# Expert rows gathered and scattered over all 128 partitions, in a mixture-of-experts kernel with streamed weights

## The chip, the cores and the metric

One core of a Trainium2 chip runs the program. The metric is device time in microseconds (us), the median of several executions. Engines: PE (TensorE, matrix products and transposes), ACT (ScalarE), DVE (VectorE), POOL (GpSimd), SP (SyncE, which here only issues DMAs). 16 DMA engines move all data between the chip's memory (HBM) and the on-chip buffer (SBUF, 128 partitions).

## The reference

A decoder layer on 1024 tokens of width 2048, in float32: input LayerNorm, a mixer (one projection, a causal convolution group and a pooling group, one projection out), LayerNorm, and a hierarchical mixture of experts (MoE), which is the part that the change touches:

```
expert = group*8 + top_i            # each token goes to 2 of 32 experts
hb = silu(xb @ w_gate[e]) * (xb @ w_up[e])   # 2048 -> 512, per expert
y  = hb @ w_down[e]                          # 512 -> 2048
out[token] += gate * y
h = layer_norm(alpha*h + out)
```

All 32 experts are used, so 32 x 12 pieces of weights of 1 MB have to be read from HBM.

## The kernel before

The program runs in three parts: the mixer (up to about 1080 us), the MoE, and the last sum and LayerNorm (from about 2175 us). The change lies in the MoE.

**Weights.** Each expert has 8 units of gate and up weights (`in_w_gu_dram`) and 4 of down weights (`in_w_dn_dram`), each a tile of 128 partitions x 2048 floats. SP loads them in the order in which PE uses them (`load_next`, L1571), into 16 slots: ten `er`, three `e2a`, and one each of `e2b`, `e2c`, `e2d` (NE2, L57). `free` (L1588) gives a slot to the next unit when PE has used it. A few tiles that are needed only later take one early unit each (`load_home`, FIRST and FIRST2, L59). An issue on SP also waits until an earlier transfer of SP's queue has landed.

**Rows.** The routing table `tabd` holds, for each expert, the token and the destination of each of its rows. `ent_load` (L1364) fetches a block's part of it as the tile `en`; `gather` (L1371) is an indirect DMA, issued by POOL, that reads the rows from `h1d` into a tile `xg`, one row of 8 KB to one partition; `scatter` (L1376) writes the finished rows to `yd`. Unfilled places carry an index out of bounds and move nothing. There are five tiles `xg` of 128 x 2048, used in turn.

**Blocks.** Experts are sorted by their number of rows, and position p of the program takes the expert of rank PERM[p] (L72), with blocks of fixed size for that rank (BLOCKS, L69): 35 blocks over 32 positions, of which 7 have 128 places, 8 have 96, 8 have 64, 3 have 48 and 9 have 32. (The first two positions, which have 64 places each, are among the 8.) So a gather names 128, 96, 64, 48 or 32 partitions.

**Steps.** `steps` (L1560) is the list that sets the order of everything: 16 half units G (gate and up) and 8 half units D (down) per position, 768 in all, the first 8 G of the next position ahead of the D of this one. At each step PE multiplies the weights with the block's transposed rows `xt`. A Part of 64 rows puts its two matmuls side by side in PE's columns, a Part of 32 rows its four (`Part.mm`, L1429). `x_quad` (L1462) transposes rows on PE, into a PSUM tile `ms`, which ACT or DVE copies to `xt`; `hidden` (L1479) applies silu and the gate; `y_out` (L1518) adds the two sums of the down product to the block's own rows in `xg`. `rows_out` (L1656) issues the gather for the block five ahead and then the scatter of the block that is done, both on POOL.

Of the kernel before, what the change touches and what calls it, by code (L numbers as in the profile page):

```python
# [26 lines left out]
NE = 32  # L27
# [15 lines left out]
NXG = 5  # L43
# [21 lines left out]
ROWS = {38: (3, 4)}  # L65
# [4 lines left out]
          + [((0, 128),)] * 4 + [((0, 96),)] * 7 + [((0, 64),)] * 5 + [((0, 48),)] * 3 + [((0, 32),)] * 8)  # L70
# [7 lines left out]
def trunk_kernel(ctx, tc, xcat, gin, bin_, grow, brow, w_in, b_in, conv_w, conv_b, cln_g, cln_b,  # L78
# [1234 lines left out]
    XG = {}  # L1313

    def xg_tiles(name, ids):
        p_ = pool(name, 1)
        for i in ids:
            XG[i] = p_.tile([P, D], F32, name=f"xg{i}")
# [4 lines left out]
    xg_tiles("xgp", (2, 3, 4))  # L1323
# [4 lines left out]
    xg_tiles("xgq", (0, 1))  # L1328
    xtp = pool("xtp", 3)
# [34 lines left out]
    def ent_load(e, start, n):  # L1364
        t = enp.tile([P, 4], I32, name="en", tag="en")
        v = tabv[start:start + n] if isinstance(start, int) else tabv[bass.ds(start, n)]
        v = v[:, e] if isinstance(e, int) else v[:, bass.ds(e, 1)].rearrange("r e c -> r (e c)")
        nc.sync.dma_start(t[:n], v)
        return t

    def gather(en, xg, n):  # L1371
        nc.gpsimd.indirect_dma_start(out=xg[:n], out_offset=None, in_=h1d,
                                     in_offset=bass.IndirectOffsetOnAxis(ap=en[:n, 0:1], axis=0),
                                     bounds_check=SEQ - 1, oob_is_err=False)

    def scatter(en, xg, n):  # L1376
        nc.gpsimd.indirect_dma_start(out=yd, out_offset=bass.IndirectOffsetOnAxis(ap=en[:n, 1:2], axis=0),  # L1377
                                     in_=xg[:n], in_offset=None, bounds_check=2 * SEQ - 1, oob_is_err=False)
# [36 lines left out]
    class Part:  # L1415
# [3 lines left out]

        def __init__(self, r0, n):  # L1420
            self.r0, self.n = r0, n
            c0 = r0 % P
            if n == 64:
                self.at = {(0, 0): c0, (1, 0): 64 - c0}
            else:
                o = 64 - c0
                self.at = {(0, 0): c0, (0, 1): c0 + 32, (1, 0): o, (1, 1): o + 32}

        def mm(self, bank, lhs, t, half, first, last):  # L1429
# [5 lines left out]
            for j, odd, h_ in sorted(order, key=lambda x: self.at[x[:2]]):  # L1435
                c = self.at[j, odd]
                nc.tensor.matmul(bank[c:c + self.n], lhs(h_)[:, self.r0:self.r0 + self.n],  # L1437
                                 t[:, h_ * 1024 + j * 512:h_ * 1024 + (j + 1) * 512],
                                 start=first and (self.n == 32 or half == 0), stop=last and half == 1)

        def sums(self, bank, j, odd=0):
            c = self.at[j, odd]
            return bank[c:c + self.n]

        def rows(self, t, c0=0, c1=512):
            return t[self.r0:self.r0 + self.n, c0:c1]

    class Block:
# [6 lines left out]

        def x_alloc(self):
            self.xt = xtp.tile([P, 16, P], F32, name="xt", tag="xt")
# [4 lines left out]
        def x_quad(self, q):  # L1462
            p_ = ms()
            m, nk = self.m, 16 // self.quads()
            pv = p_[:, :nk * m].rearrange("p (k n) -> p k n", k=nk)
# [3 lines left out]
            xv = self.xt[:, nk * q:nk * q + nk, :m]  # L1469
            if q % 2:  # L1470
                nc.vector.tensor_copy(xv, pv)
            else:
                nc.scalar.activation(xv, pv, AF.Copy)

        def gu(self, u, t, half):
            for part, bank in zip(self.parts, self.gb):
                part.mm(bank, lambda h_: self.xt[:, 2 * u + h_, :], t, half, u == 0, u == 7)

        def hidden(self):  # L1479

            m = self.m
            sg = hbp.tile([P, 512], F32, name="sg", tag="sg")
            ul = hbp.tile([P, 512], F32, name="dt", tag="dt")
            odd = [p_ for p_ in self.parts if p_.n == 32]
            for part, bank in zip(self.parts, self.gb):
                if part.n == 64:
                    nc.scalar.activation(part.rows(sg), part.sums(bank, 0), AF.Silu)
                else:
                    t = hbp.tile([P, 1024], F32, name="od", tag="od", bufs=1)
                    nc.scalar.activation(part.rows(t), part.sums(bank, 0, 1), AF.Copy)  # L1490
                    nc.scalar.activation(part.rows(t, 512, 1024), part.sums(bank, 1, 1), AF.Copy)
                nc.scalar.activation(part.rows(ul), part.sums(bank, 1), AF.Copy)
            for part, bank in zip(self.parts, self.gb):
                if part.n == 32:
                    nc.vector.tensor_tensor(part.rows(sg), part.rows(t), part.sums(bank, 0), op=OP.add)
                    nc.vector.tensor_tensor(part.rows(ul), part.rows(ul), part.rows(t, 512, 1024), op=OP.add)
            yield
            for part in odd:
                nc.scalar.activation(part.rows(sg), part.rows(sg), AF.Silu)
                yield  # L1500
            nc.vector.scalar_tensor_tensor(sg[:m], sg[:m], self.en[:m, 2:3].bitcast(F32), ul[:m],
                                           op0=OP.mult, op1=OP.mult)
            for _ in range(YX):
                yield
            p_ = ms()
            for k in range(4):
                nc.tensor.transpose(p_[:, k * m:(k + 1) * m], sg[:m, k * P:(k + 1) * P], ident[:m, :m])
            self.ht = hbp.tile([P, 512], F32, name="hth", tag="hth")
            nc.scalar.activation(self.ht[:, :4 * m], p_[:, :4 * m], AF.Copy)

        def down(self, u, t, half):

            m = self.m
            for part, bank in zip(self.parts, self.pds[u // 2]):
                part.mm(bank, lambda h_: self.ht[:, (2 * (u % 2) + h_) * m:(2 * (u % 2) + h_ + 1) * m], t, half,
                        u % 2 == 0, u % 2 == 1)

        def y_out(self, dp):  # L1518
            m, c = self.m, 1024 * dp
            t = hbp.tile([P, 512], F32, name="dt", tag="dt")  # L1520
            for part, bank in zip(self.parts, self.pds[dp]):
                xs = part.rows(self.xg, c, c + 512)
                nc.scalar.activation(part.rows(t), part.sums(bank, 1), AF.Copy)  # L1523
                if part.n == 32:
                    o = hbp.tile([P, 1024], F32, name="od", tag="od", bufs=1)
                    nc.scalar.activation(part.rows(o), part.sums(bank, 0, 1), AF.Copy)
                    nc.scalar.activation(part.rows(o, 512, 1024), part.sums(bank, 1, 1), AF.Copy)
                nc.vector.scalar_tensor_tensor(xs, xs, ALPHA / 2, part.sums(bank, 0), op0=OP.mult, op1=OP.add)  # L1528
                if part.n == 32:
                    nc.vector.tensor_tensor(xs, xs, part.rows(o), op=OP.add)  # L1530
                    nc.vector.tensor_tensor(part.rows(t), part.rows(t), part.rows(o, 512, 1024), op=OP.add)
            xs = self.xg[:m, c + 512:c + 1024]
            nc.vector.scalar_tensor_tensor(xs, xs, ALPHA / 2, t[:m], op0=OP.mult, op1=OP.add)  # L1533
# [3 lines left out]
    FIN = [(len(ALL) - 1 - d) % NXG for d in (4, 3)]  # L1537
    for m, (p, b) in enumerate(ALL):
        b.xg = XG[m % NXG]
    next_ent, next_gather = [0], [0]  # L1540

# [35 lines left out]
    def load_home(home):  # L1577
# [4 lines left out]
        t = xtp.tile([P, 2048], F32, name="xt", tag="xt") if home == "x" else XG[home]  # L1582
# [16 lines left out]
    def x_early(p):  # L1599

        return POS[p + 1][:3 - len(POS[p])] if p + 1 < NE else []
# [10 lines left out]
    nc.gpsimd.memset(XG[0], 0.0)  # L1612
    ents(2)
    gathers(1)
# [22 lines left out]
    def first_rows(ms_):  # L1637

        for m in ms_:
            nc.gpsimd.memset(XG[m], 0.0)  # L1640
            gathers(m + 1)

    first_rows((1, 2))
# [12 lines left out]
    def rows_out(p):  # L1656

        if p:
            gathers(ndone[0] + NXG)
        ndone[0] += len(POS[p])  # L1660
        for b in POS[p]:
            scatter(b.en, b.xg, b.n)
# [5 lines left out]
    for n, (kind, p, k) in enumerate(steps):  # L1668
        if n in ROWS:
            first_rows(ROWS[n])  # L1670
# [42 lines left out]
        while rows and (rows[0][0] <= n or n + 1 == len(steps)):  # L1713
            rows_out(rows.popleft()[1])
# [8 lines left out]
        if (kind, p, k) == ("D", NE - 2, 0):  # L1723
            nc.sync.dma_start(XG[FIN[0]], bc(lf_g, 0, D))
            nc.sync.dma_start(XG[FIN[1]], bc(lf_b, 0, D))
# [6 lines left out]
    with tc.For_i(0, nov, 1) as it:  # L1732
# [5 lines left out]
        blk.en, blk.xg, blk.gb, blk.pds = ent_load(e, st, P), XG[(len(ALL) - 1) % NXG], PB6[:2], [PB6[2:4], PB6[4:]]  # L1738
        gather(blk.en, blk.xg, P)
# [15 lines left out]
        scatter(blk.en, blk.xg, P)  # L1755
# [5 lines left out]
    fg, fb = XG[FIN[0]], XG[FIN[1]]  # L1761
# [160 lines left out]
```

## Time and profile before

| | us |
|---|---|
| median of 3 runs | 2276.13 (2275.77 to 2277.64) |
| the profiled execution | 2279.34 |
| its span, first to last instruction | 2277.5 |

The profiled execution's own time is 1.8 us more than its span and 3.2 us above the median of the runs.

The page of the profile gives busy times per engine, then the span in 40 slices of 57 us: a digit is the busy share in tenths, PEclk the granted TensorE clock in tenths of full speed, DMA the mean busy share of the 16 DMA engines, and GB/s what they moved. The view of stretches gives the same for any interval, and the view of waits says who waited for whom. In a row, `xg<-h1d,en` means that `xg` is written from `h1d` and `en`; `x16` is a count.

### The profile page before, as it was taken

How to read it: one execution, taken by the hardware profiler on the slowest of the kernel's cores; microseconds unless marked ns; L12 is line 12 of the kernel's file. 1: busy time of each engine (PE TensorE's matmuls, PEld its weight loads, DVE VectorE, ACT ScalarE, POOL GpSimd, SP SyncE). 2: the span in 40 equal slices, each digit the busy share in tenths (PEclk: the TensorE clock that was granted, in tenths of full speed). 3: DMA queues.
4: the chain of work that ended last, by engine and by line, in shares of the span. 5: the costliest groups of instructions: out<-in, count | busy, mean ns of one | idle time of the engine just before them, and what ended most of it. 6: DMA issues, size and time to landing. Idle time of an engine off the chain costs nothing. (4 is left out here: it accounts for less than half of the span.)

```text
span 2277.5 us, 29748 instructions
## 1 busy us (share of the span) xinstructions
PE 2011.4 (88%) x11015; PEld 1170.3 (51%) x11015; DVE 1130.0 (50%) x1918; ACT 746.1 (33%) x1308; POOL 670.7 (29%) x536
## 2 busy tenths in 40 slices
PE   5899999999999989987699999999979998999900
PEld 4799999978877867766232232223312222233300
DVE  8678767768856696796242212222111123131269
ACT  5633334324433444453112211222211122221255
POOL 5566757635222354264210001000000000000045
PEclk8999999999999999999799999999989998999955
DMA  6211121123565665678899999999999999989984
GB/s 206 96 56 56 56 66 56 56 79 104 208 199 166 226 224 210 218 261 306 310 374 416 405 393 393 400 413 411 356 399 398 408 416 392 402 323 418 420 329 163
DMA packets 132916, 614.29 MB, mean 270 GB/s; under 512 B 21216, under 2 KB 27872, under 8 KB 78368
## 3 DMA queue, kind: packets, MB, share of 16 engines
q1 hardware_dynamic: 124480, 570.37, 66.0%
q0 software_dynamic: 6848, 33.60, 4.2%
q10 hardware_dynamic: 1440, 8.39, 0.9%
q8 instruction: 88, 1.44, 0.3%
q14 instruction: 60, 0.49, 0.1%
HBM read 570.11 MB, written 51.36 MB: 273 GB/s over the span
## 5 line engine op out<-in xcount | busy, mean ns | idle before, releaser
L1437 PE MATMUL mm<-er,xt 128*64 128x512 f32 (+1 forms) x2120 | 420.7, 612 | 20.0 <-DMA er<-in_w_gu_dram 19.9
L754 PE MATMUL mm<-hl,whi 128*128 128x256 f32 (+2 forms) x1152 | 359.5, 324 | 0.6 <-POOL hl L343 0.6
L753 PE MATMUL mm<-hh,whi 128*128 128x256 f32 (+2 forms) x1152 | 347.3, 326 | 0.4 <-ACT l L589 0.4
L1528 DVE SCALAR_TENSOR_TENSOR xg<-xg,mm 64x512 f32<-64x512 f32 (+1 forms) x100 | 68.1, 681 | 515.6 <-ACT dt L1523 364.5
L373 POOL TENSOR_TENSOR wlo<-raw,whi 128x512 fp32r<-128x512 f32 x129 | 176.5, 1369 | 405.9 <-ACT whi L372 341.0
L1377 POOL DMA_INDIRECT yd<-xg,en x35 | 33.1, 945 | 798.3 <-DVE xg L1533 675.5
L758 PE MATMUL mm<-hh,wlo 128*128 128x256 f32 (+2 forms) x1152 | 258.1, 323 | 1.9 <-POOL wlo L373 1.9
L1437 PEld LDWEIGHTS mm<-er,xt 128*64 128x64 f32 (+1 forms) x2120 | 109.3, 128 | 275.1 <-issue 221.3
L372 ACT ACTIVATE whi<-raw 128x512 fp32r<-128x512 f32 x252 | 156.6, 627 | 271.3 <-PE mm L754 138.2
L412 DVE SCALAR_TENSOR_TENSOR ms<-l,cwt,ms 128x512 f32<-128x512 f32 x352 | 232.5, 749 | 0.0
L754 PEld LDWEIGHTS mm<-hl,whi 128*128 128x128 f32 x1152 | 219.0, 190 | 18.7 <-POOL hl L343 1.0
L753 PEld LDWEIGHTS mm<-hh,whi 128*128 128x128 f32 x1152 | 219.2, 190 | 3.4 <-ACT l L589 0.8
L758 PEld LDWEIGHTS mm<-hh,wlo 128*128 128x128 f32 x1152 | 193.6, 190 | 37.0 <-POOL wlo L373 2.9
L1437 PE MATMUL mm<-er,hth 128*64 128x512 f32 (+1 forms) x1032 | 201.9, 611 | 7.0 <-DMA er<-in_w_dn_dram 6.9
L1523 ACT ACTIVATE dt<-mm 64x512 f32<-64x512 f32 (+1 forms) x100 | 59.1, 591 | 364.7 <-PE mm L1437 350.9
L1219 PE MATMUL mm<-wlo,yh 128*128 128x512 f32 x392 | 156.2, 399 | 11.1 <-DVE wlo L373 10.9
L1218 PE MATMUL mm<-whi,yh 128*128 128x512 f32 x392 | 158.2, 404 | 1.6 <-ACT whi L372 1.6
L1220 PE MATMUL mm<-whi,yl 128*128 128x512 f32 x392 | 155.4, 396 | 0.0
L428 POOL TENSOR_TENSOR l<-l,t 128x512 f32<-128x512 f32 x112 | 141.8, 1295 | 0.0
L1437 PEld LDWEIGHTS mm<-er,hth 128*64 128x64 f32 (+1 forms) x1032 | 55.2, 129 | 152.9 <-issue 123.3
L373 DVE TENSOR_TENSOR wlo<-raw,whi 128x512 fp32r<-128x512 f32 x123 | 103.3, 851 | 56.6 <-ACT whi L372 54.9
L1437 PE MATMUL mm<-e2a,xt 128*64 128x512 f32 (+1 forms) x536 | 102.9, 599 | 1.1 <-DMA e2a<-in_w_gu_dram 1.1
(347 smaller groups left out, 2752.2 us busy)
## 6 DMA issues: line engine op xcount, KB each, us to landing
er<-in_w_gu_dram SPq DMA_DIRECT2D x161, 1024.0 KB, 19.8
er<-in_w_dn_dram SPq DMA_DIRECT2D x77, 1024.0 KB, 19.4
e2a<-in_w_gu_dram SPq DMA_DIRECT2D x47, 1024.0 KB, 20.7
raw<-in_w_out_dram SPq DMA_DIRECT2D x70, 512.0 KB, 4.4
raw<-in_w_in_dram SPq DMA_DIRECT2D x56, 512.0 KB, 3.3
e2a<-in_w_dn_dram SPq DMA_DIRECT2D x25, 1024.0 KB, 19.3
e2c<-in_w_gu_dram SPq DMA_DIRECT2D x16, 1024.0 KB, 20.6
e2d<-in_w_gu_dram SPq DMA_DIRECT2D x15, 1024.0 KB, 21.7
```

The costliest lines, as they stand in the source:

```text
L372: nc.scalar.activation(h, src, AF.Copy)
L373: self.lo(s).tensor_tensor(l, src, fr(h), op=OP.subtract)
L412: nc.vector.scalar_tensor_tensor(a, src, w, a, op0=OP.mult, op1=OP.add)
L428: nc.gpsimd.tensor_tensor(a, a, t, op=OP.add)
L753: nc.tensor.matmul(o, wh[:, ks], hh[q][:, kk, a0:a1], start=k == 0, stop=False)
L754: nc.tensor.matmul(o, wh[:, ks], hl[q][:, kk, a0:a1], start=False, stop=False)
L758: nc.tensor.matmul(o, wl[:, ks], hh[q][:, kk, a0:a1], start=False, stop=k == 15)
L1218: nc.tensor.matmul(po[t_], a_, wh, start=n == 0, stop=False)
L1219: nc.tensor.matmul(po[t_], a_, wl, start=False, stop=False)
L1220: nc.tensor.matmul(po[t_], b_, wh, start=False, stop=n == 15)
L1437: nc.tensor.matmul(bank[c:c + self.n], lhs(h_)[:, self.r0:self.r0 + self.n], t[:, h_ * 1024 + j * 512:h_ * 1024 + (j + 1) * 512], start=fi ...
L1528: nc.vector.scalar_tensor_tensor(xs, xs, ALPHA / 2, part.sums(bank, 0), op0=OP.mult, op1=OP.add)
```

## The change

Blocks of up to 64 places (m = 64 or 32) get narrow tiles `xgn` of 128 x 1024, three of them; larger blocks keep tiles `xgw` of 128 x 2048, also three. A narrow block's row is cut into f pieces, 2 for m = 64 and 4 for m = 32, and piece c of row r lies at partition c*m + r. `fetch` works out the indices f*index + c on DVE (tile `ex`), and then one gather names all 128 partitions and pieces of 4 or 2 KB. A 96-row block is gathered with 128 places, whose last 32 carry the out-of-bounds index. Blocks of 48 places now have 64. `x_quad` transposes 128 x 128 pieces in a narrow block (8 or 4 transposes in place of 16). `y_out` works on 64 partitions for a narrow block, and the 32-row Parts add their two halves in one pass (`added`). Gathers are issued every fourth step, at the earliest 8 steps after the scatter from the same tile, and for wide tiles not before step 42. The space that comes free holds a 17th weight slot `e2e`, and the wide tiles take three early units.

```diff
-NXG = 5
+NXW, NXN, NXG = 3, 3, 5
-NE2 = {"a": 3, "b": 1, "c": 1, "d": 1}
-FIRST, FIRST2 = ("a", "a", "a", "c", "d", "x"), ("b", "er", "er", 3, 4)
+NE2 = {"a": 3, "b": 1, "c": 1, "d": 1, "e": 1}
+FIRST, FIRST2 = ("a", "a", "a", "c", "d", "e", "x"), ("b", "er", "er", 0, 1)
-ROWS = {38: (3, 4)}
+WSTEP = 42
...
-    def gather(en, xg, n):
-        nc.gpsimd.indirect_dma_start(out=xg[:n], out_offset=None, in_=h1d,
-                                     in_offset=bass.IndirectOffsetOnAxis(ap=en[:n, 0:1], axis=0),
...
+    def gather(idx, xg, f=1):
+        nc.gpsimd.indirect_dma_start(out=xg[:, :D // f], out_offset=None,
+                                     in_=h1d if f == 1 else h1d.rearrange("t (c d) -> (t c) d", c=f),
+                                     in_offset=bass.IndirectOffsetOnAxis(ap=idx[:, 0:1], axis=0),
...
+        def added(self, bank):
+            o = hbp.tile([P, 512], F32, name="od", tag="od", bufs=1)
+            c = 64 - self.r0
+            nc.scalar.activation(self.pair(o), bank[c:c + 64], AF.Copy)
+            nc.vector.tensor_tensor(self.pair(o), self.pair(o), self.pair(bank), op=OP.add)
+            return self.rows(o), o[self.r0 + 32:self.r0 + 64]
...
         def x_quad(self, q):
+            if self.f == 1:
...
+            else:
+                m, nk = P, 4
+                pv = p_.rearrange("p (k n) -> p k n", k=nk)
+                xv = self.xt[:, 512 * q:512 * q + 512].rearrange("p (k n) -> p k n", k=nk)
...
         def y_out(self, dp):
+            a = ALPHA / 2
+            if self.f > 1:
+                part, bank, o = self.parts[0], self.pds[dp][0], 64 * dp
+                here, there = slice(o, o + 64), slice(64 - o, 128 - o)
+                xs = self.xg[here, :D // self.f]
+                t = hbp.tile([P, 512], F32, name="dt", tag="dt")
+                nc.scalar.activation(t[here], bank[there], AF.Copy)
+                xh = xs[:, (dp if self.f == 2 else 0) * 512:][:, :512]
+                nc.vector.scalar_tensor_tensor(xh, xh, a, bank[here], op0=OP.mult, op1=OP.add)
+                if self.f == 2:
+                    xo = xs[:, (1 - dp) * 512:][:, :512]
+                    nc.vector.scalar_tensor_tensor(xo, xo, a, t[here], op0=OP.mult, op1=OP.add)
+                else:
+                    nc.vector.tensor_tensor(xs, xs, t[here], op=OP.add)
+                return
...
+        def fetch(self):
+            self.idx = self.en
+            if self.f > 1:
+                self.idx = enp.tile([P, 2], I32, name="ex", tag="ex")
+                for c in range(self.f):
+                    nc.vector.tensor_scalar(self.idx[c * self.m:(c + 1) * self.m], self.en[:self.m, 0:2], self.f, c,
+                                            op0=OP.mult, op1=OP.add)
+            gather(self.idx, self.xg, self.f)
+            self.come = True
...
-    def gathers(upto):
+    def gathers(n, upto):
         while next_gather[0] < min(upto, len(ALL)):
             b = ALL[next_gather[0]][1]
-            gather(b.en, b.xg, b.n)
+            if sent.get(b.place, -99) + 8 > n or b.f == 1 and n < WSTEP:
+                return
+            if b.place not in sent:
+                nc.gpsimd.memset(b.xg, 0.0)
+            b.fetch()
+            sent[b.place] = NONE
...
     for n, (kind, p, k) in enumerate(steps):
-        if n in ROWS:
-            first_rows(ROWS[n])
+        if n % 4 == 2:
+            gathers(n, min(ndone[0] + NXG, next_ent[0]))
```

How the instructions move, first on POOL's queue around positions 11 to 14, in the middle of the MoE. A row is a source line, an operation, and out<-in with the shape of the output; `yd` is the target of a scatter. Before:

```order
L1372 DMA xg_10328<-h1d,en 96x2048
L1372 DMA xg_10329<-h1d,en 32x2048
L1377 DMA yd<-xg_10330,en 2048x2048
L1372 DMA xg_10330<-h1d,en 128x2048
L1377 DMA yd<-xg_10346,en 2048x2048
L1372 DMA xg_10346<-h1d,en 64x2048
L1377 DMA yd<-xg_10347,en 2048x2048
L1372 DMA xg_10347<-h1d,en 32x2048
```

The same blocks with the change:

```order
L1379 DMA xgw_10329<-h1d,en 128x2048
L1379 DMA xgn_10351<-h1d,ex 128x512
L1385 DMA yd<-xgn_10349,ex 4096x1024
L1379 DMA xgw_10330<-h1d,en 128x2048
L1385 DMA yd<-xgw_10328,en 2048x2048
L1379 DMA xgn_10349<-h1d,ex 128x1024
L1385 DMA yd<-xgn_10350,ex 4096x1024
L1379 DMA xgn_10350<-h1d,ex 128x512
```

The order is the same here; every gather now names 128 partitions, and those of narrow blocks have rows of 1024 or 512 floats.

On DVE, the last two `y_out` pairs before the overflow list's count (`novt`) is read, at the end of the MoE. Before:

```order
L1528 SCALAR_TENSOR_TENSOR xg_10330<-xg_10330,mm 32x512
L1530 TENSOR_TENSOR xg_10330<-xg_10330,od 32x512
L1531 TENSOR_TENSOR dt<-dt,od 32x512
L1533 SCALAR_TENSOR_TENSOR xg_10330<-xg_10330,dt 32x512
L1528 SCALAR_TENSOR_TENSOR xg_10330<-xg_10330,mm 32x512
L1530 TENSOR_TENSOR xg_10330<-xg_10330,od 32x512
L1531 TENSOR_TENSOR dt<-dt,od 32x512
L1533 SCALAR_TENSOR_TENSOR xg_10330<-xg_10330,dt 32x512
L1730 TENSOR_LOAD novt
```

With the change:

```order
L1564 SCALAR_TENSOR_TENSOR xgn_10350<-xgn_10350,mm 64x512
L1569 TENSOR_TENSOR xgn_10350<-xgn_10350,dt 64x512
L1564 SCALAR_TENSOR_TENSOR xgn_10350<-xgn_10350,mm 64x512
L1569 TENSOR_TENSOR xgn_10350<-xgn_10350,dt 64x512
L1807 TENSOR_LOAD novt
```

Two DVE instructions in place of four follow each half of the last block's down product; on ACT, one copy (L1562) takes the place of three (L1523, L1526, L1527).

On PE, the last position's transposes. Before:

```order
L1437 MATMUL mm<-e2a,xt 32x512 x8
L1468 MATMUL ms<-ident,xg_10330 128x32 x16
L1437 MATMUL mm<-e2c,xt 32x512 x4
L1437 MATMUL mm<-e2d,xt 32x512 x4
L1437 MATMUL mm<-e2b,xt 32x512 x4
```

With the change:

```order
L1447 MATMUL mm<-er,xn 32x512 x8
L1502 MATMUL ms<-ident,xgn_10350 128x128 x4
L1447 MATMUL mm<-er,xn 32x512 x12
L1447 MATMUL mm<-e2a,xn 32x512 x8
L1543 MATMUL ms<-ident,sg 128x32 x4
```

Four transposes of 128 x 128 stand where sixteen of 32 rows stood.

## Rows read from the trace of the kernel before

**Rows 1.** The page: DMA share in tenths and GB/s, in 40 slices.
```profile
DMA  6211121123565665678899999999999999989984
GB/s 206 96 56 56 56 66 56 56 79 104 208 199 166 226 224 210 218 261 306 310 374 416 405 393 393 400 413 411 356 399 398 408 416 392 402 323 418 420 329 163
```

**Rows 2.** Stretches of the MoE; columns as in the first line.
```profile
core 0: us, PE busy (x) PEld busy (x) DVE busy (x) ACT busy (x) POOL busy (x), PEclk, DMA share, GB/s
1104.00:1140.00 36.00, 36.00 (x178) 12.80 (x177) 4.69 (x7) 5.04 (x8) 2.30 (x3) 0.94 0.93 338
1140.00:1930.00 790.00, 735.67 (x4013) 222.13 (x4013) 183.41 (x327) 162.05 (x285) 54.53 (x55) 0.97 1.01 398
1930.00:2167.00 237.00, 227.67 (x1296) 73.92 (x1292) 52.33 (x79) 52.00 (x92) 10.53 (x11) 0.99 0.96 391
```

**Rows 3.** SP's waits for PE, 1140 to 1930 and 1930 to 2167.
```profile
SPq L1361 <- PE mm L1437: 11.9, 23, 2.3
...
SPq L1361 <- PE mm L1437: 135.3, 63, 5.8
```

**Rows 4.** PE's longest waits, 1104 to 2170: us, times, longest.
```profile
PE mm L1437 <- DMA er<-in_w_gu_dram: 19.9, 18, 4.3
PE ms L1507 <- DVE sg L1501: 11.7, 8, 3.3
```

**Rows 5.** Stretches: a 64-place gather, a scatter, a 128- and a 96-place gather.
```profile
1451.20:1455.00 3.80, 3.80 (x23) 0.93 (x20) 0.00 (x0) 0.00 (x0) 0.00 (x0) 1.00 1.06 250
1441.80:1445.40 3.60, 3.60 (x20) 0.85 (x21) 1.27 (x2) 1.20 (x3) 0.00 (x0) 1.00 1.00 419
1416.00:1421.00 5.00, 5.00 (x26) 1.71 (x24) 1.81 (x3) 1.12 (x2) 0.00 (x0) 1.00 1.01 419
1308.60:1314.00 5.40, 5.40 (x32) 1.45 (x28) 0.00 (x0) 0.39 (x1) 0.00 (x0) 1.00 1.04 267
```

**Rows 6.** POOL in order of time: the three gathers of group 5.
```profile
1304.27 0.97 POOL L1372 DMA_INDIRECT xg<-h1d,en  x1 [8.28 <-DMA yd<-xg,en]
...
1411.63 1.02 POOL L1372 DMA_INDIRECT xg<-h1d,en  x1 [7.35 <-DMA er<-in_w_gu_dram]
...
1446.92 0.95 POOL L1372 DMA_INDIRECT xg<-h1d,en  x1 [8.40 <-issue]
```

**Rows 7.** DMA queues from 1451.2 to 1455: packets, MB, share; q0 is POOL's.
```profile
q0 software_dynamic: 69, 0.40, 45.3%
```

**Rows 8.** Two stretches of the long middle, columns as in group 2.
```profile
1300.00:1425.00 125.00, 124.86 (x682) 38.04 (x684) 23.52 (x36) 23.67 (x42) 8.63 (x9) 1.00 1.01 394
1425.00:1720.00 295.00, 263.31 (x1420) 82.61 (x1417) 63.46 (x95) 58.42 (x102) 18.74 (x20) 0.95 1.01 397
```

**Rows 9.** PE in order of time: start, us; transposes, one wait.
```profile
1335.89 0.71 PE L1468 MATMUL ms<-ident,xg 64*128 64x64 f32 x8
...
1350.97 0.63 PE L1507 MATMUL ms<-ident,sg 128*128 128x128 f32 x4
...
2144.32 1.18 PE L1468 MATMUL ms<-ident,xg 32*128 32x32 f32 x16
...
2151.55 0.40 PE L1507 MATMUL ms<-ident,sg 32*128 32x32 f32 x4 [1.63 <-DVE sg L1501]
```

**Rows 10.** The end of the MoE in order of time: PE, ACT, DVE.
```profile
2167.70 2.42 PE L1437 MATMUL mm<-e2d,hth 128*32 128x512 f32 x8
...
2171.38 0.59 ACT L1527 ACTIVATE od<-mm 32x512 f32<-32x512 f32 x1
...
2174.03 0.68 DVE L1533 SCALAR_TENSOR_TENSOR xg<-xg,dt 32x512 f32<-32x512 f32 x1
```

**Rows 11.** The gathers, all 35: duration on POOL, and time to landing.
```profile
L1372 POOL DMA_INDIRECT xg<-h1d,en x35: 924/965/1402, 1094.4 to 2056.4; - x35
...
DMA to landing us min/median/max: 6.3/9.8/15.7
```

**Rows 12.** A small DVE instruction, 1082.59 us.
```profile
1082.59 0.16 DVE L1068 SCALAR_TENSOR_TENSOR ds<-rr,eid 128x4 int32<-128x4 f32 x1
```

More of the change, by code (lines that the diff above doesn't have):

```diff
@@ L1312, in trunk_kernel, with xg_tiles @@
     pool = lambda n_, b_: moe.enter_context(tc.tile_pool(name=n_, bufs=b_, reuse_waits="tile"))
-    XG = {}
-    def xg_tiles(name, ids):
+    XW, XN = {}, {}
+    def xg_tiles(name, to, n, w):
         p_ = pool(name, 1)
-        for i in ids:
-            XG[i] = p_.tile([P, D], F32, name=f"xg{i}")
+        for i in range(n):
+            to[i] = p_.tile([P, w], F32, name=f"{name}{i}")
     e2 = {"a": pool("e2a", NE2["a"])}
-    xg_tiles("xgp", (2, 3, 4))
+    xg_tiles("xgw", XW, NXW, D)
     e2["b"] = pool("e2b", NE2["b"])
@@ L1421, in __init__, with at, mm @@
             self.r0, self.n = r0, n
[L1422 to L1429, printed above, removed]
+        def at(self, j, odd=0, flip=0):
+            if self.n == 64:
+                return (self.r0 + 64 * j) % P
+            return (self.r0 + 64 * (odd ^ flip)) % P + 32 * j
+        def mm(self, bank, lhs, t, half, first, last, flip=0):
             if self.n == 64:
@@ L1483, in hidden @@
             ul = hbp.tile([P, 512], F32, name="dt", tag="dt")
-            odd = [p_ for p_ in self.parts if p_.n == 32]
+            both = {}
             for part, bank in zip(self.parts, self.gb):
@@ L1487, in hidden @@
                     nc.scalar.activation(part.rows(sg), part.sums(bank, 0), AF.Silu)
+                    nc.scalar.activation(part.rows(ul), part.sums(bank, 1), AF.Copy)
                 else:
[L1489 to L1496, printed above, removed]
+                    both[part] = part.added(bank)
             yield
-            for part in odd:
-                nc.scalar.activation(part.rows(sg), part.rows(sg), AF.Silu)
+            for part, (g_, u_) in both.items():
+                nc.scalar.activation(part.rows(sg), g_, AF.Silu)
+                nc.scalar.activation(part.rows(ul), u_, AF.Copy)
                 yield
@@ L1529, in y_out @@
-                if part.n == 32:
-                    nc.vector.tensor_tensor(xs, xs, part.rows(o), op=OP.add)
-                    nc.vector.tensor_tensor(part.rows(t), part.rows(t), part.rows(o, 512, 1024), op=OP.add)
-            xs = self.xg[:m, c + 512:c + 1024]
-            nc.vector.scalar_tensor_tensor(xs, xs, ALPHA / 2, t[:m], op0=OP.mult, op1=OP.add)
+                    y0, y1 = part.added(bank)
+                else:
+                    y0, y1 = part.sums(bank, 0), part.sums(bank, 1)
@@ new lines, in y_out @@
+                nc.scalar.activation(part.rows(t), y1, AF.Copy)
+                nc.vector.scalar_tensor_tensor(xs, xs, a, y0, op0=OP.mult, op1=OP.add)
+            xs = self.xg[:m, c + 512:c + 1024]
+            nc.vector.scalar_tensor_tensor(xs, xs, a, t[:m], op0=OP.mult, op1=OP.add)
+        def fetch(self):
[7 more added lines that the diff above has]
+            self.come = True
@@ L1535, in trunk_kernel, with send @@
+        def send(self):
+            scatter(self.idx, self.xg, self.m if self.f == 1 else P, self.f)
     POS = [[Block(*b) for b in ((FBLK,) if p < len(STAT) else BLOCKS[PERM[p]])] for p in range(NE)]
     ALL = [(p, b) for p in range(NE) for b in POS[p]]
-    FIN = [(len(ALL) - 1 - d) % NXG for d in (4, 3)]
-    for m, (p, b) in enumerate(ALL):
-        b.xg = XG[m % NXG]
+    ring = {}
+    for p, b in ALL:
+        w = b.f == 1
+        i = ring.get(w, 0)
+        b.place = (w, i % (NXW if w else NXN))
+        b.xg = (XW if w else XN)[b.place[1]]
+        b.come = False
+        ring[w] = i + 1
@@ L1540, in trunk_kernel @@
+    FIN = [XW[(ring[True] + d) % NXW] for d in range(2)]
+    SPARE = XW[(ring[True] + 2) % NXW]
     next_ent, next_gather = [0], [0]
+    sent = {}
     def ents(upto):
@@ L1635, in trunk_kernel @@
             b.x_quad(q)
[L1637 to L1643, printed above, removed]
+    load_home(2)
+    gathers(0, NXG)
     chain = deque()
@@ L1654, in trunk_kernel, with rows_out @@
     rows = deque()
-    def rows_out(p):
-        if p:
-            gathers(ndone[0] + NXG)
+    def rows_out(p, n):
         ndone[0] += len(POS[p])
         for b in POS[p]:
-            scatter(b.en, b.xg, b.n)
+            b.send()
+            sent[b.place] = n
     def quads(bs):
```

85 lines of the change are left out of this document (52 added, 33 removed).

## The prediction

> **What bounds the kernel now.** I read the page first. In its 40 slices [rows 1] the DMA digit stands at 9 from slice 21 on, up to the last two slices but for one 8: that is the MoE, which streams some 400 MB of weights. There GB/s is not constant although the engines are always busy: it lies between 323 and 420. So a busy DMA moves less in some slices than in others, and that is the place to look.
>
> The stretches of the MoE [rows 2] show two regimes. From 1140 to 1930 DMA is busy throughout (1.01) at 398 GB/s, and PE works 735.7 of 790 us. From 1930 to 2167 PE works 227.7 of 237. Which of the two sets the pace is told by the waits of SP, which issues the weights [rows 3]: up to 1930 it waited for PE, that is for a free slot, 11.9 us in all, and after 1930 135.3 us. So DMA paces the first 790 us and PE the last 237. PE's own waits [rows 4] agree: the longest kind is for weights. Something that makes DMA faster is paid out before 1930 as PE idle time that vanishes; after 1930 only less work on PE pays.
>
> Why is GB/s uneven? I laid narrow stretches over single transfers of POOL [rows 5, 6]. While the 64-place gather issued at 1446.92 ran, DMA was as busy as ever and moved 250 GB/s; the 96-place gather issued at 1304.27 gave 267. The 128-place gather issued at 1411.63 gave 419, and a scatter of 96 places also 419. In the slow stretch most of the traffic is weights (the gather's queue q0 has 45.3% of the engines' time and 0.40 MB [rows 7]), so the weights are slowed with it. The reader is to see that the loss goes with gathers that name fewer than 128 partitions, 28 of the 35, and not with scatters and not with full gathers.
>
> **The change, part by part.** The sum is made against the profiled execution, 2279.3 us, which is 3.2 above the median of the runs.
>
> 1. *All gathers name 128 partitions.* If the slow stretches vanish, the 790 us run at the 419 GB/s of a full gather [rows 5]: 790 x 398/419 = 750.4, so 39.6 us less DMA time. PE must be able to take it: it idles 54.3 us there [rows 2], and at most 11.7 of those are waits for the gate product on DVE [rows 4], so 42.6 are left, just enough. They are not where the savings are: from 1300 to 1425 PE idles 0.1 us while DMA would save 125 x (1 - 394/419) = 7.5; from 1425 to 1720 PE idles 31.7 and DMA would save 15.5 [rows 8]. So 7.5 us have to be carried on as weights that land early, three units of 1.05 MB. Slots are free for that, since SP hardly waits for PE [rows 3]. I give back 2.6 for imperfect carrying and take 37; the ends are 0 and 40.
>
> 2. *The opening, 1104 to 1140* [rows 2], ran at 338 GB/s with PE at 36 of 36. At 419 it would save 7.0 us of DMA time, which again only builds a lead. Part of it is small loads that stay. I take 3, between 0 and 7.
>
> 3. *Less work on PE and a shorter chain.* A 64-row block transposes in 2 x 0.71 us, a 32-row block in 1.18; a set of four 128 x 128 transposes takes 0.63 [rows 9], so they become 1.26 and 0.63. Before 1930 that is covered by DMA. After it, one 64-row and three 32-row blocks are transposed: 0.16 + 3 x 0.55 = 1.8 us. In `hidden` a 32-row block had three ACT copies, two DVE adds and the silu ahead of the gate; now one copy, one add, the silu and a copy. With 0.59 and 0.68 us apiece [rows 10] that is 1.2 shorter, and PE waited 1.63 for this chain in one of the last blocks [rows 9]; for two such blocks I take 2.2. I take 4, between 0 and 6.
>
> 4. *The 17th slot.* Where DMA paces, a free slot is no shortage; where PE paces, a fuller store changes nothing. I take 0. The upper end is one unit at 419 GB/s, 2.5 us, if PE's last waits for weights go.
>
> 5. *The end.* After the last matmul (2170.1) come three ACT copies up to 2171.97 and four DVE instructions up to 2174.71, then the last scatter [rows 10]. One copy and two DVE instructions stay: 2 x 0.59 + 2 x 0.68 = 2.5 us less, on the path that sets the end.
>
> 6. *What is added.* Indices: 11 x 2 + 9 x 4 = 58 small DVE instructions of about 0.16 us [rows 12], 9 us; DVE works 183 of 790 us [rows 2], which hides them. They wait for `en`; in program order that load is issued at least 66 steps (at 790 us for some 570 steps, 90 us) ahead, and SP trails by at most the 34 steps of 17 units, so nothing queues up on DVE. Only at the very start does PE wait for the first gather behind two of them: 0.5 us. Gathers come later than before on POOL's queue, but the shortest distance from issue to the first transpose is 17 steps, 23 us, against a longest landing of 15.7 [rows 11]. More places cost POOL nothing that shows: an issue takes 0.92 to 1.40 us over all sizes now [rows 11]. The pieces of 4 and 2 KB have no row under a full DMA. From below their price is 0; from above I take slice 12 [rows 1], where loads have 4 KB rows and less: 199 GB/s at a share of 0.6 is 332, and 288 if the digit hides 0.69, so up to 45% dearer. At most 992 narrow rows go both ways, 16.3 MB or 39 us, so up to 18 us. I take 1, since those slices are nearer to idle gaps than to a full queue.
>
> Sum: 37 + 3 + 4 + 0 + 2.5 - 0.5 - 1 = 45. The profiled execution would take 2234, the median 2276.1 - 45 = **2231**.
>
> **The rivals.**
>
> *The 96-row blocks stay slow.* Their gathers name 128 places, but still write the same 96 partitions. If the loss comes from which partitions are written, those eight keep it: 5.4 x (1 - 267/419) = 1.96 us each [rows 5], 15.7 in all, which gives 2247. Against it: the rows that filled the 128-place gathers need not have filled every place either. The Trainium skill says in "SBUF — State Buffer", section "Door 1: The DMA port swizzle", that DMA bandwidth hangs on how many of 16 ports the partitions reach; by that rule the partitions written are what counts, and this rival would hold. No row separates the two. 0.11.
>
> *Pieces are dear.* The upper end of step 6 and a poor carry together leave less than half, 45 - 17 - 7.5 = 20.5: 2256. 0.05.
>
> *Nothing happens on the DMA.* The slow stretch might come from another property of small gathers, such as their place in the traffic. Then steps 3, 5 and 6 remain: 6 us, 2270, just beyond what counts as no change. The Trainium skill has a rule against the change, in "DMA: Bandwidth & Descriptors", section "Rules for kernel authors": transfers to one half of the partitions spread over all 16 engines anyway, so splitting work between halves brings nothing. By it the time would be this rival's; the 250 against 419 GB/s in the trace speak against reading it so. 0.06, half of it within the bound of no change.
>
> *Slower: the loss is per piece.* Place: every narrow gather. The 64-place one lost 3.8 x (1 - 250/419) = 1.5 us [rows 5] for 0.40 MB, 49 rows [rows 7]: 31 ns a row. If each piece disturbs the weights as a row does now, narrow blocks with 992 places become 2560 pieces: 79 us in place of 31 when full, 32 more at two thirds full; less 6 that gives 2302. It turns slower than before once a piece loses more than about half of what a row loses. For it: the loss grows with the gather. Against it: 128-place gathers have the most rows and lose nothing. 0.05.
>
> **How the numbers follow.** Forecast 0.70, from 2220 (40 + 7 + 6 + 2.5 + 2.5 - 0.5 is 57.5, a little less in practice) to 2245; better than that 0.03; the rivals 0.11, 0.05, 0.06 and 0.05. The range of 8 in 10 is 2217 to 2256: it takes in the two rivals that lose a part and leaves out no change and slower. A measurement here tells about 0.2% (4.6 us) from no change: faster 0.92, same 0.03, slower 0.05.
>
> **What would show it.** Right: GB/s near 419 in every MoE slice in which DMA is at 9 until PE paces; SP's waits for PE begin well before 1930; PE idle from 1140 on falls from 54 to under 20 us; the last chain after the last matmul is 2.5 us shorter. A 96-row gather at 419 excludes the first rival, one at 267 confirms it. Wrong: stretches near 260 GB/s that are as long as before or longer, new waits of PE for `xg` tiles or for DVE behind the index instructions, or a PE that is busy throughout with less than 30 us gained.

## The result, and the profile after

The changed kernel takes 2225.65 us (2224.59 to 2228.39, four runs) against 2276.89 of the kernel before beside it: a ratio of 0.9774, interval 0.976 to 0.9789, or 51 us less. In a later comparison it was 0.9785 (0.9772 to 0.9799).

The page of the kernel after, DMA share and GB/s in slices of 55.7 us, which answers to [rows 1]:

```profile
DMA  6211112114555667577999999999999999989983
GB/s 204 97 65 50 56 57 67 58 53 128 195 185 179 205 197 258 187 250 275 334 418 420 420 418 415 418 416 418 415 409 420 411 415 411 418 359 420 420 341 155
```

From slice 21 on GB/s lies between 409 and 420 wherever DMA is at 9 (in the slice with 359 it is at 8); before, it fell to 356 in the long middle in a slice with DMA at 9. The stretches of the MoE, which answer to [rows 2]:

```profile
core 0: us, PE busy (x) PEld busy (x) DVE busy (x) ACT busy (x) POOL busy (x), PEclk, DMA share, GB/s
1104.00:1140.00 36.00, 34.83 (x158) 12.78 (x160) 5.54 (x11) 5.22 (x8) 3.06 (x4) 0.92 1.01 413
1140.00:1880.00 740.00, 712.70 (x3844) 211.43 (x3840) 160.63 (x317) 132.02 (x232) 61.25 (x63) 0.99 1.01 416
1880.00:2120.00 240.00, 232.51 (x1304) 75.19 (x1304) 46.75 (x76) 44.98 (x79) 12.11 (x12) 1.00 0.98 404
```

The opening runs at 413 GB/s instead of 338, the long middle at 416 instead of 398, with PE idle 27.3 us in it instead of 54.3: less than before, but not under 20, as the prediction's sign had it. SP's waits for PE, 1140 to 1880 and then 1880 to 2120:

```profile
SPq L1365 <- PE mm L1447: 34.0, 41, 6.4
...
SPq L1365 <- PE mm L1447: 119.9, 56, 5.7
```

In the middle SP waits for a free slot three times as long as before (34.0 against 11.9 us [rows 3]): weights land early more often, as they must if a lead is carried. PE's waits, 1104 to 2120, against [rows 4]:

```profile
PE mm L1447 <- DMA er<-in_w_gu_dram: 10.4, 11, 2.9
PE ms L1543 <- DVE sg L1537: 8.8, 9, 1.6
```

For two kernels to be compared step by step a clock is needed that both share. The 4800 weight matmuls of the MoE are the same in number and order in every kernel here, so I take the stretch from the start of the first to that of number 4650 and call it the same work. Before, and then after:

```profile
1104.56:2143.36 1038.80, 980.56 (x5312) 302.72 (x5315) 230.32 (x397) 208.52 (x364) 66.36 (x67) 0.97 1.00 394
```

```profile
1107.00:2096.59 989.59, 959.49 (x5133) 292.47 (x5136) 204.80 (x392) 174.76 (x305) 74.44 (x77) 0.99 1.01 413
```

49.2 us are gained in this work: 28.1 as PE idle time and 21.1 as PE busy time, the latter at a granted clock of 0.99 against 0.97, and with 179 fewer transposes (some 15 us of it lie in the weight matmuls, 5 in the transposes). The stretch begins 2.4 us later, 2.0 of which stood before the MoE already. Behind it, the last 150 matmuls take 22.90 us instead of 26.76.

The end in order of time, which answers to [rows 10]:

```profile
2118.47 1.06 PE L1447 MATMUL mm<-er,hth 128*32 128x512 f32 x8 [1.46 <-SPq L1809]
2119.65 0.59 ACT L1562 ACTIVATE dt<-mm 64x512 f32<-64x512 f32 x1 [3.64 <-PE mm L1447]
...
2121.00 0.69 DVE L1569 TENSOR_TENSOR xgn<-xgn,dt 64x512 f32<-64x512 f32 x1
2123.58 0.99 POOL L1385 DMA_INDIRECT yd<-xgn,ex  x1 [6.63 <-DMA yd<-xgn,ex]
```

From the last matmul's end (2119.53) to the end of the last DVE instruction it is 2.16 us, against 4.59 before (2170.12 to 2174.71). But POOL issues the scatter only 1.89 us later, where it took 0.28 before: it sat idle for 6.63 us, and what came last was the landing of the scatter before it. So 1.6 us of what the shorter chain saves are lost to that landing.

### The profile page after: what moved, and what is told of

Its sections match the earlier page's. It is cut to its first block, busy times and chain, and to the rows that moved or that the text cites. A ratio compares the mean times of both kernels' runs of the same rounds, so it can differ in the third digit from the quotient of the medians.

```text
span 2226.6 us, 29205 instructions
## 1 busy us (share of the span) xinstructions
PE 1993.2 (90%) x10819; PEld 1164.5 (52%) x10819; DVE 1098.7 (49%) x1905; ACT 706.6 (32%) x1239; POOL 672.9 (30%) x545
## 3 DMA queue, kind: packets, MB, share of 16 engines
q10 hardware_dynamic: 1440, 8.39, 0.9%
## 5 line engine op out<-in xcount | busy, mean ns | idle before, releaser
L1447 PE MATMUL mm<-er,xt 128*64 128x512 f32 (+1 forms) x1056 | 212.4, 601 | 0.9 <-DMA er<-in_w_gu_dram 0.9
L1447 PE MATMUL mm<-er,hth 128*32 128x512 f32 (+1 forms) x992 | 185.8, 606 | 4.4 <-DMA er<-in_w_dn_dram 2.8
L1564 DVE SCALAR_TENSOR_TENSOR xgn<-xgn,mm 64x512 f32<-64x512 f32 x40 | 27.4, 685 | 256.4 <-ACT dt L1562 242.8
L1447 PE MATMUL mm<-er,xn 128*64 128x512 f32 (+1 forms) x744 | 143.0, 613 | 9.5 <-DMA er<-in_w_gu_dram 9.5
L1385 POOL DMA_INDIRECT yd<-xgn,ex x20 | 20.2, 1012 | 401.2 <-DVE xgn L1567 220.1
L1580 DVE SCALAR_TENSOR_TENSOR xgw<-xgw,mm 64x512 f32<-64x512 f32 x44 | 30.1, 683 | 208.4 <-ACT dt L1579 207.3
L1385 POOL DMA_INDIRECT yd<-xgw,en x15 | 14.6, 973 | 373.2 <-DVE xgw L1582 316.2
L1447 PEld LDWEIGHTS mm<-er,xt 128*64 128x64 f32 (+1 forms) x1056 | 55.5, 128 | 132.5 <-issue 119.7
```

What stands on the lines that cost most here:

```text
L1385: nc.gpsimd.indirect_dma_start(out=yd if f == 1 else yd.rearrange("t (c d) -> (t c) d", c=f), out_offset=bass.IndirectOffsetOnAxis(ap=idx[ ...
```

## The experiments

**Only the places, in two forms.** Does naming 128 partitions alone give the gain? To the kernel before:

```diff
-        nc.gpsimd.indirect_dma_start(out=xg[:n], out_offset=None, in_=h1d,
-                                     in_offset=bass.IndirectOffsetOnAxis(ap=en[:n, 0:1], axis=0),
+        nc.gpsimd.indirect_dma_start(out=xg, out_offset=None, in_=h1d,
+                                     in_offset=bass.IndirectOffsetOnAxis(ap=en[:, 0:1], axis=0),
```

with the out-of-bounds index in the rest of `en`, set on POOL, in the first form ahead of the load of `en`, in the second ahead of the gather.

> The kernel before, with one thing of the change: every gather names 128 partitions, the places beyond the block's own carrying the out-of-bounds index; no pieces, no narrow tiles, no 17th slot, same transposes and sums. Theory (the number of places that a gather names decides): GB/s near 416 in the MoE wherever DMA is busy throughout, and nearly the whole gain of the change without its slot and its shorter PE work: 2276 less 37 to 43, that is 2233 to 2239. Rival (the partitions that rows are written to decide, or the spread in pieces does): narrow blocks still write 32 to 64 partitions, the stretches at 250 to 270 GB/s stay, 2273 to 2279.

> As the kernel before with all gathers naming 128 partitions, but the out-of-bounds index is written on POOL directly ahead of the gather, so that no load on SP waits for POOL (there a load of en waited for it, ahead of the weights). Theory: the run with places alone gained only about 27 us up to the last unit because SP was held up behind POOL: at 1380 to 1400 and 1590 to 1605 us DMA fell to 312 to 372 GB/s right after such loads. Then 2242 to 2248 now. Rival: with clean gathers PE paces more stretches and the kernel before has neither the shorter PE work nor the fuller opening to use the rate: no different from that run, 2252 to 2257, with the same dips.

Measured: 2254.97 us, 0.9897 (0.9881 to 0.9912), and 2254.32, 0.9896 (0.9881 to 0.9911). Both are 24 us better than before, nearly half of the gain, and between what theory and rival expected of the first; the order on POOL made no difference, so the theory of the second falls too. The slow stretches are gone all the same: rows of 8 KB in POOL's queue take 0.313 us on average in the stretch of the same work, 0.365 before, 0.312 after. The same work in the second form:

```profile
1106.24:2117.92 1011.68, 971.53 (x5309) 301.84 (x5312) 230.38 (x397) 208.50 (x364) 73.26 (x118) 0.98 0.99 404
```

404 GB/s, not 413, at a lower share of DMA. The next two rows show where the share goes, in stretches behind two gathers of 64-row blocks (issued at 1581.22 and 1587.91):

```profile
1592.00:1594.50 2.50, 2.50 (x14) 0.86 (x12) 2.13 (x4) 0.99 (x3) 0.00 (x0) 1.00 0.57 223
1597.00:1599.00 2.00, 2.00 (x19) 0.97 (x16) 0.50 (x1) 0.00 (x0) 1.02 (x2) 1.00 0.71 221
```

```profile
SPq L1361 <- DMA e2a<-in_w_gu_dram: 10.5, 3, 4.4
```

SP (here its waits from 1586 to 1602) waited for weights to land, up to 4.4 us at once, while by the packets of the trace 7 to 14 of 16 engines were at work. So a part of the engines was behind and the others had nothing left to do. Summed over the stretch of the same work, the packets' time over 16 engines and the engines' idle time are: before 1035 and 17.5 us, places alone 1002 and 22.3, after 995 and 8.5 (packets overlap a little, so the two don't add up to the stretch's 1039, 1012 and 990). Naming 128 places takes 33 us of work away and adds 5 of idleness; the rest of the change takes 8 more of work and 14 of idleness.

**96-row blocks by 96 and by 112 places,** in the changed kernel, all else kept (the second has 112 where 96 stands in the call):

```diff
-            gather(self.idx, self.xg, self.f)
+            gather(self.idx, self.xg, self.f, 96 if self.m == 96 else P)
```

> The changed kernel, with its eight 96-row blocks gathered by 96 places again. Theory (places named): their stretches fall back to about 267 GB/s, 1.96 us lost at each, at most 15.7 in all; those in stretches that PE paces cost less, so 2226 plus 8 to 16: 2234 to 2242. Rival (partitions written): the same 96 partitions are written either way, so 2226 within 2 us and 416 GB/s throughout.

> The changed kernel, with its eight 96-row blocks gathered by 112 places in place of 128. With 96 places the same blocks cost 15 us. Theory: a gather is clean only when it names all 128 partitions, so 112 lose nearly as much as 96: 8 to 15 us. Rival: the loss falls with the share of places that is missing, 64 to 250 GB/s, 96 to 267: at 112 under 8 us. Second rival: 112 are enough, no loss.

Measured: 2242.92 us, 0.9841 (0.9827 to 0.9854), and 2243.41, 0.9856 (0.9841 to 0.9871). One gather of 80 rows, the same in all, by 128, 112 and 96 places:

```profile
1839.50:1843.70 4.20, 4.20 (x24) 0.93 (x20) 0.00 (x0) 0.00 (x0) 0.00 (x0) 1.00 1.01 416
```

```profile
1849.50:1854.70 5.20, 5.20 (x32) 1.09 (x28) 0.08 (x1) 0.59 (x1) 0.00 (x0) 1.00 1.03 301
```

```profile
1850.70:1855.70 5.00, 5.00 (x28) 1.20 (x32) 0.00 (x0) 0.23 (x1) 0.00 (x0) 1.00 1.05 280
```

The rows go to the same 80 partitions each time; 416 GB/s become 301 and 280. In the same work the two runs lose 15 and 16 us against the change. The number of places named decides, and 112 of 128 are no better than 96.

**Two gathers of 64 places for each gather,** in the changed kernel, where a gather now names 64 places from the partition given last (0 or 64):

```diff
+            hi = enp.tile([P, 2], I32, name="eh", tag="eh")
+            nc.vector.tensor_copy(hi[:64], self.idx[64:, 0:2])
             gather(self.idx, self.xg, self.f)
+            gather(hi, self.xg, self.f, 64)
```

> The changed kernel, with each gather issued as two gathers of 64 places, one for the lower and one for the upper half of the partitions (the upper indices copied on DVE to a tile that begins at partition 0); rows, bytes, pieces and partitions written are the same. Theory (places named in one gather): the loss of the 64-place gather before, 31 ns a row of 8 KB or 3.8 us per MB, comes back for all 16.8 MB of rows, 63 us of DMA time, of which stretches paced by PE hide a part: 2265 to 2290, with GB/s near 250 while the halves run. Rival (all 128 partitions being filled, in whatever number of gathers): 2226 to 2230.

Measured: 2303.73 us, 1.0108 (1.0093 to 1.0124): 25 us slower than before, and above the theory's range. While the two halves of a 128-row gather run (issued at 1411.62 and 1412.88):

```profile
1414.50:1428.00 13.50, 13.50 (x72) 3.99 (x68) 2.13 (x3) 3.87 (x7) 0.00 (x0) 1.00 1.03 264
```

The same rows, pieces and partitions cost 75 us more in the same work. The theory's 63 was a little low: the packets' time over 16 engines grew by 79, and PE hid little of it.

**Without the 17th slot.**

```diff
-NE2 = {"a": 3, "b": 1, "c": 1, "d": 1, "e": 1}
+NE2 = {"a": 3, "b": 1, "c": 1, "d": 1}
```

> The changed kernel without the 17th weight slot. Theory of the prediction (the slot is worth nothing where DMA paces): 2226 within 1 us. Rival, from the trace after: DMA stood partly idle from 1085 to 1095 us, and the slot's first unit is loaded just ahead of that gap, so that one unit of 1.05 MB less is moved behind 1105 us: without the slot plus 2.5 us, 2228 to 2229, and the distance to the kernel before is smaller by 2.5 us already at the fourth scatter.

Measured: 2231.03 us, 0.9791 (0.9777 to 0.9804); the change itself has 0.9774 and 0.9785. In the same work next to nothing tells from the slot: 990.8 us, against 989.6 and, in the second run of the change, 990.5. The rival's 2.5 us don't show at the fourth scatter; the early lead it pointed to is there without the slot. But this work ends at matmul 4650. The last 150 matmuls, without the slot and then with it:

```profile
2096.32:2123.24 26.92, 20.84 (x168) 5.26 (x160) 8.09 (x12) 6.51 (x12) 1.97 (x2) 0.91 0.98 405
```

```profile
2096.63:2119.53 22.90, 18.69 (x168) 5.34 (x160) 8.08 (x12) 6.51 (x12) 1.97 (x2) 1.00 1.00 414
```

Without the slot they take as long as in the kernel before (26.76 us), with it 4.0 less; in the second run of the change they take 22.74. PE waits there 2.8 us for the down weights in `e2a`, against 0.6 for those in `er` with the slot, and its granted clock is 0.91 in place of 1.00. So by the traces the slot is worth some 4 us at the end. By the medians it is 1 to 4, and their intervals overlap.

**The units issued into the idle stretch, and the tail.** First `FIRST` ends with `"x", 0, 1`; then the chain of the last `hidden` also rests from the fifth down step of the block before:

```diff
-        if k != 15:
+        if k != 15 and not (kind == "D" and p == NE - 2 and k > 4):
```

> The changed kernel, with the first two early units of the wide tiles issued ahead of the loads of en instead of behind them, into the stretch from 1085 to 1095 us in which DMA stood at 0.68 to 0.75. Theory: some 3 us of DMA time are used that were idle, and since DMA paces the next hundred us the whole MoE ends 2 to 3 us earlier: 2223 to 2224. Rival: the loads of en land behind 2 MB of weights, the first gather comes later and PE starts its MoE later by up to 5 us; the lead in weights pays that back only in part: 2226 to 2229.

> The same two units issued early, and in the last position the four transposes of hidden come behind the last down unit of the block before, so that its rows are scattered earlier. Theory: in the run of the change the last scatter was issued 1.9 us after its rows were done, because it waits until the scatter before it has landed; with that one 1.5 us earlier the end comes 1 to 1.6 us earlier than in the run with the two early units alone. Rival: the last scatter waits for something else, the end is the same, or PE's waiting for the transposed hidden rows costs 1 us.

Measured: 2231.29 us, 0.9795 (0.9781 to 0.9808), and 2234.04, 0.9805 (0.9792 to 0.9819): no gain from either. SP in order of time, first run:

```profile
1074.61 0.33 SPq L1365 DMA_DIRECT2D xt<-in_w_dn_dram  x1
1088.32 0.33 SPq L1365 DMA_DIRECT2D xgw<-in_w_dn_dram  x1
1089.12 0.33 SPq L1365 DMA_DIRECT2D xgw<-in_w_gu_dram  x1
1089.54 0.57 SPq L1374 DMA_DIRECT2D en<-tabd  x1
```

The tile was not free before 1088, so the units came too late for the gap, and PE waited 26.0 us for its first gather instead of 21.2. In the second run the next-to-last scatter went out 1.2 us earlier than in the first (2115.60 against 2116.82), the last 0.8 (2123.47 against 2124.29), 0.3 of which stood at matmul 4650 already: within the whole kernel nothing of it shows.

**The change again, without its third early unit, and with the transposes made as long as before,** on one chip:

```diff
-    load_home(2)
...
+            more = {1: [], 2: [0] * (q == 0), 4: [0, 1, 2, 3]}[self.f]
-            for kk in range(nk):
+            for kk in more + list(range(nk)):
```

> The changed kernel as it is, for comparison on the chip of the three runs beside it: 0.9774 of the kernel before, within 0.0015.

> The changed kernel, without the early unit in the third wide tile (the kernel before had two early units, the change has three). Theory: that unit stands between the loads of en on SP at 1102 us and keeps DMA busy where the kernel before drained (98 to 162 GB/s from 1110 to 1115 us); without it DMA idles 2 to 3.5 us in the opening, as in the kernel before, and the time is 2 to 3.5 us longer. Rival: the next slot's load takes its place at once, and the time differs by less than 1 us.

> The changed kernel, with transposes repeated so that a narrow block's take PE as long as before: one more 128 x 128 transpose for a 64-row block, four more for a 32-row block; the products are the same. Added are 11 x 0.16 + 9 x 0.63 = 7.4 us of PE. Theory of the prediction (before PE paces, this is hidden under DMA): only those behind 1930 us count, 2 us. Rival: PE paces several stretches by now (PE at 100% in 1271 to 1429 and 1488 to 1579), so most of it counts, 5 to 7.4 us.

Measured: 2229.09 us, 0.9785 (0.9772 to 0.9799), without the unit 2227.42, 0.9781 (0.9768 to 0.9794), with the longer transposes 2227.95, 0.9785 (0.9771 to 0.9798). None differs by more than its interval, which is some 3 us to either side. From 1105 to 1115 us, the change and then without the unit:

```profile
1105.00:1115.00 10.00, 9.55 (x38) 4.03 (x40) 1.60 (x5) 0.60 (x1) 3.06 (x4) 0.76 1.02 398
```

```profile
1105.00:1115.00 10.00, 10.00 (x41) 3.31 (x42) 1.73 (x5) 0.59 (x1) 3.06 (x4) 0.83 0.78 245
```

The unit does fill DMA, as its theory said, and the same work takes 2.9 us longer without it, within the 2 to 3.5 expected. In that trace PE starts on the weights 2.4 us earlier (1104.93 against 1107.30), which hides it, but this is not the unit's doing. PE's first transposes, with their wait for the first gather, in the change and then without the unit:

```profile
1105.45 1.94 PE L1502 MATMUL ms<-ident,xgn 128*128 128x128 f32 x8 [20.75 <-DMA xgn<-h1d,ex]
```

```profile
1103.10 1.94 PE L1502 MATMUL ms<-ident,xgn 128*128 128x128 f32 x8 [20.79 <-DMA xgn<-h1d,ex]
```

The wait is the same; PE was done with the mixer 2.4 us earlier. That moment lies between 1080 and 1085 us over the kept traces, and so a total tells less of the MoE than the same work does. What the unit is worth in total stays open.

The longer transposes don't show either. PE's rows hold 4 us more for them (24.2 against 20.0 us), less than the 7.4 reckoned. The rival's 5 to 7.4 are excluded; of the theory's 2 the medians can't tell, but the traces speak against it: the same work takes 990.1 us, with 45 more transposes, against 990.5. The run with them is 1.9 us behind at 1580 us and takes 2.1 less in the next 112, where PE is idle 1.4 us less: what they delay PE by in one stretch, it waits less for weights in a later one.

**Eight of the 64-row blocks whole again,** named by 128 places:

```diff
+        if b.m == 64 and p > 2:
+            b.f = 1
```

A fourth wide tile takes the place of the 17th slot.

> The changed kernel, in which eight of the eleven 64-row blocks are whole again: rows of 8 KB on the first 64 partitions, in wide tiles, with 128 places named and the upper 64 empty. A fourth wide tile takes the place of the 17th slot. Theory: the run that only named 128 places stayed 24 us behind the change because rows on a part of the partitions load a part of the 16 DMA engines (7 to 9 of 16 were at work from 1592.5 to 1594 us there, after two such gathers), while SP waits for the weights behind them; then the eight blocks bring back a third to a half of it, 8 to 14 us, 0.9820 to 0.9845 of the kernel before, with packets as short as now (0.31 us) but DMA below 0.9 after such gathers. Rival: what was missing there lay elsewhere (shorter sums, the moment of the gathers, the opening), and whole rows with 128 named places cost nothing: 0.9785 within 0.0015.

Measured: 2246.65 us, 0.986 (0.984 to 0.988), 17 us above the change. In the same work it loses 8.5, 999.07 us against 990.5:

```profile
1116.37:2115.44 999.07, 962.55 (x5197) 294.34 (x5200) 201.08 (x376) 174.80 (x305) 75.62 (x85) 0.99 1.00 408
```

Another 9.1 lie ahead of it: the first gather goes out later (1105.60 against 1096.46). SP shows why: the load of slot `e2c` had to wait for the routing table here and went out at 1092.38, in the change at 1070.56, so that three units of weights stand just ahead of the list `en` which that gather needs (on DVE `ex`, which is made from it, begins 10.6 us after the issue of that load, in the change 2.5). And 4.1 lie behind it: the last 150 matmuls take 26.9 us, as without the 17th slot, which this run has given up. So of the total, which is above the theory's range, nothing follows. The slot told nothing in the same work, so the 8.5 go with the whole rows as far as the runs tell; they are at the lower end of the theory, with 3.8 more of idle engines and 4.3 more of packet time. The Trainium skill, in "DMA: Bandwidth & Descriptors", section "The descriptor swizzle", gives for a transfer to 128 partitions the engine of each partition: partitions 0 to 63 lie on eight engines, in groups of four, and 64 to 127 on the other eight. By that rule, with the gathered rows of the 35 blocks counted in the trace, the busiest engine would carry 223 rows of 8 KB with places alone, 196 with these eight blocks whole and 172 with the change; at 0.31 us a row, 16 and 7.5 us more than the change, an estimate. The traces agree as far as they go: 21.2 and 8.5 us in the same work. No record here names a packet's engine, so that the uneven load is the cause is argued, not shown.

## Why the prediction came out right, and where its division was wrong

How far ahead of the kernel before each run is, from its own first matmul on (us; matmul 1500 is at 1440 us before):

| at matmul | 450 | 750 | 1500 | 1800 | 2700 | 3300 | 4650 |
|---|---|---|---|---|---|---|---|
| places alone | 4.6 | 9.5 | 9.5 | 16.2 | 25.9 | 24.7 | 27.1 |
| change, 96 by 96 | 4.7 | 12.0 | 12.9 | 21.4 | 30.9 | 31.2 | 34.1 |
| change | 5.0 | 12.3 | 13.3 | 25.4 | 43.3 | 43.6 | 49.2 |

- *Step 1, 37 us.* The mechanism is shown (96, 112 and twice 64 places), and the lead was carried over the stretch that PE paces: from 750 to 1500 it stands still, then it is paid out. But the sentence "If the slow stretches vanish, the 790 us run at the 419 GB/s of a full gather" failed: with places alone they vanish, and the gain is 27 us in the same work and 24 in all. Gathers that name 128 places but fill few of them leave engines idle. The step took the cut into pieces as a mere price; eight 64-row blocks without it lose 8.5. Nor is the gain paid out as vanished PE idle time alone: 21.1 of the 49.2 us are shorter PE work, some 15 of them the same weight matmuls at the higher granted clock, for which the step had no term.
- *Step 2, 3 us.* About 5 by matmul 450, in the upper half of its bounds; this takes in the first 72 us of step 1, and the two can't be told apart there. The third early unit fills DMA in the opening and is worth 2.9 us of the same work; in the total that is not shown.
- *Step 3, 4 us.* The transposes' 1.8 don't show (nothing is lost when they are made longer). PE's waits for the gate product fell from 11.7 to 8.8 us, those of the last blocks from 1.63 to 1.08: about 1 in place of 2.2.
- *Step 4, 0 us.* Too low. In the same work it is right, to some 1 us, but in the last 150 matmuls the slot takes 4.0 us away, where the step gave at most 2.5 for "PE's last waits for weights".
- *Step 5, 2.5 us.* The chain is 2.4 shorter, but only 0.8 of it reaches the end; the step overlooked that the last scatter waits for the one before, which was hidden under the longer chain.
- *Step 6.* Packets of 4 KB take 0.163 us (a piece of 4 KB, or, as packets of 2 KB hardly occur, two of 2 KB), twice that is 0.326 against 0.312 for 8 KB: 2114 packets x 0.007 / 16 = 0.9 us, as taken (1). That they even the load was missing.

So that the sum (45 against 51) came out near is in part luck. A loss that step 1 missed in the places was made good by pieces that step 6 booked as a cost, and the slot, booked at nothing, gave about what steps 3 and 5 gave less than booked. One reading of the page was off without touching the argument: the 323 GB/s stand in a slice with DMA at 8; where it is at 9, GB/s lay between 356 and 420.

The rivals: the 96-row blocks are not slow, and the run with 96 places shows what they would have cost, 15 us where 15.7 were worked out; which partitions are written does not decide whether packets are slow. The rule of the Trainium skill that stood beside it ("SBUF — State Buffer", "Door 1: The DMA port swizzle") does not order these runs: the same ports give 280, 301 and 416 GB/s. By its own table partitions 0 to 95 reach all 16 ports, so it did not bear the rival out as the prediction said. The Trainium skill's other rule ("DMA: Bandwidth & Descriptors", "Rules for kernel authors") was not against the change either: it ends in the advice to use one transfer over 128 partitions, which agrees with the 75 us that two gathers of 64 places cost here. Pieces are not dear. "Nothing happens on the DMA" and the loss per piece are excluded by 416 GB/s. Not settled: why a packet takes longer when a gather names fewer than 128 places, and how the 13 us of the same work between places alone and the change that the eight blocks don't account for divide among 32-row pieces, the new moments of the gathers and the shorter sums.

## What to carry to other kernels

Look for a busy DMA whose GB/s varies, and lay narrow stretches over single transfers: here small gathers slowed all traffic by more than a third while they ran. Name all 128 partitions in one gather and spread the rows evenly over them; naming alone gave half. Before booking a saving on one engine, lengthen that work and measure: the transposes' time did not show. And a stretch of the same work has an end; look behind it too, where the slot's 4 us lay.

## What the runs showed of the hardware

- A gather by 112 places moved 301 GB/s together with the weights, by 96 280, by 128 416, for the same 80 rows; two gathers of 64 places in place of one of 128 rows 264. Packets of 8 KB, of the weights as well as of the rows, took 0.45, 0.49 and 0.31 us meanwhile.
- With 128 places named and the rows on a part of them, packets keep their 0.31 us, but DMA fell to shares of 0.57 and 0.71 for 2 to 2.5 us while SP waited for weights to land.
- In this program a scatter to `yd` follows the landing of the scatter before it: the last one went out 1.89 us after its rows were done, POOL having been idle for 6.63 us.
